# Compression's inputs loaded ahead, and the late modulation's rows on another queue

## The chip, the cores and the metric

The kernel runs on one core of one Trainium2 chip. The metric is the device time of one execution in microseconds (us); lower is better. Three executions of the kernel before took 2179.93, 2182.69 and 2183.15 us, with a median of 2182.69 us. A difference of under 0.2% can hardly be told from none here.

## The reference

Two transformer blocks follow each other, for one sequence of 512 tokens of width 1024, all in float32. Only the first block's mixer matters for the change. In short:

```python
mod = silu(c) @ ada_w + ada_b                     # 6 x 1024 numbers for the whole sequence
sh_m, sc_m, g_m, sh_f, sc_f, g_f = split(mod, 6)
h = rmsnorm(x, norm_g[0]) * (1 + sc_m) + sh_m
p = h @ w_in                                      # 1024 -> all mixers' inputs
y_a = rwkv7_mix(...)                              # a recurrent scan, 4 heads
y_b = fox_mix(...)                                # causal attention, 6 heads
y_c = nsa_mix(...)                                # attention over compressed, chosen and near keys, 6 heads
    # inside: for t in (kc, vc): blocks of 32 tokens, a step of 16, so 31 blocks
    #   flat = (block + pe).reshape(31, 2 groups, 2048); t_cmp = gelu(flat @ w1) @ w2
y = concat([y_a, y_b, y_c]) @ w_out
x = x + g_m * rmsnorm(y, norm_g[1])
h = rmsnorm(x, norm_g[2]) * (1 + sc_f) + sh_f     # the feed-forward block follows
```

The first two of the six parts of `mod` are needed at once. The other four (`g_m`, `sh_f`, `sc_f`, `g_f`), called the late modulation here, are needed only when the mixer's output is added to x.

## The kernel before, in words

Activations lie transposed in SBUF: 128 features on the partitions, 512 tokens along them. TensorE's products are made in three passes of split float32 (`whi`, `wlo` against `uh`, `ul`). The weights come as one stream of blocks of 128x1024 numbers (512 KB): `Weights.load` (L263) takes one of three buffers `raw` and loads it on SP's queue, and `Weights.next` (L273) splits it into `whi` (ScalarE, L278) and `wlo` (VectorE, L279), after which the buffer is free.

The program is written as Python generators that are stepped in turn. At build time a planner then orders the instructions of every engine: it takes them by their place in the program, and a later one ahead of an earlier one when its buffers and inputs are ready by the planner's own reckoning. On the chip each engine, and SP's queue of loads too, works through its list in that fixed order. So a load that is written late and waits for nothing can stand early.

The stages around the change:

- **The first stage** (0 to about 73 us) makes the early modulation and the first projection (L527 to L604). Its loads run on SP's queue (L531, L558, L269).
- **prep** (L750) makes the recurrent scan's inputs for two halves, t = 0 and 1, and between its steps the first `NA` = 5 projections are filled in (L1163 to L1165), among them `kcv[0]` and `kcv[1]`, the inputs of compression.
- **The core stage** (L1179 to L1193) steps the two scans (`core`, L823) 32 times. In each turn it fills in about 2.2 projection steps (L1183) from the other ten projections, takes three steps (L1187) of a side list (compression, then the three pairs of fox heads, then `stacks`), and in every second turn calls `some_ada` (L1186).
- **some_ada** (L621) does one of 16 rows of the late modulation: two loads of 512 KB on SP's queue into `raw`, the same three buffers that the weights use (L630, L631), then on GpSimd four multiplications and additions for each (L635, L637, L638) into `am`. One row later two small products with ones on TensorE (L644) and an addition (L646) finish a row. `some_ada(99)` (L1193) finishes what is left.
- **compress** (L1013) works for keys, then values. For each of two groups it copies a part of `kcv` into `kk2`, shifted by one token in the lower half (L1020, L1021, on SP's queue), and VectorE adds the position term into `kr` (L1025). Four loads of `w1` of 256 KB (L1029) each serve four products (L1032). All of `kr`, `kk2` and `w1` take the five buffers called `e` of the scan.
- **The selected and window attention** (`nsa`, L1217) follows, and the first part of the output projection is filled in between its steps.

The late results `ks`, `kw` and `nq0` to `nq2` (L509, L510) and `fq`, `fk` (L515) have tiles of their own in the pool `keep`, which exist from the start, although they are written only by the last projections of the core stage.

Of the kernel before, what the change touches and what calls it, by code (L numbers as in the profile page):

```python
# [255 lines left out]
class Weights:  # L256


    def __init__(self, nc, pool, src, raw_bufs, bufs):
        self.nc, self.pool, self.src, self.raw_bufs, self.bufs = nc, pool, src, raw_bufs, bufs  # L260
        self.i = 0
# [22 lines left out]
def two_blocks(ctx, tc, ins, out):  # L284
# [224 lines left out]
    ks, kw = [keep.tile([P, T], F32, name=n) for n in ("ks", "kw")]  # L509
    nq = [keep.tile([P, T], F32, name=f"nq{j}") for j in range(3)]  # L510
# [4 lines left out]
    fq, fk = [[keep.tile([P, T], F32, name=f"f{c}{j}", tag=f"f{c}{j}") for j in range(3)] for c in "qk"]  # L515
# [104 lines left out]

    def some_ada(n=1):  # L621

        for _ in range(n):
            if not todo and not owing:
                return
            if todo:
                sec, k = todo.pop(0)
                am = st.tile([P, 256], F32, name="am", bufs=4)
                for q in range(2):
                    aw = wpool.tile([P, 4, 256], F32, name="raw", bufs=W.raw_bufs)  # L630
                    nc.sync.dma_start(aw.rearrange("p a b -> p (a b)"), ins["ada"][sec, k][:, q * 1024:(q + 1) * 1024])  # L631
                    for r in range(4):
                        s = sil[:, 4 * q + r:4 * q + r + 1]
                        if q + r == 0:
                            G.tensor_scalar(am, aw[:, r], s, 1.0, op0=MUL, op1=MUL)  # L635
                            continue
                        G.tensor_scalar(aw[:, r], aw[:, r], s, 1.0, op0=MUL, op1=MUL)  # L637
                        G.tensor_tensor(am, am, aw[:, r], op=ADD)  # L638
# [310 lines left out]
    def copy_to(dst, scale=1.0):  # L949
        return lambda ps: act(dst, ps, AF.Copy, scale=scale)  # L950
# [3 lines left out]
    jobs = [proj_t("nsa", copy_to(kcv[0])), proj_t("nsa", copy_to(kcv[1])), proj_n("nsa_n", 280, 2, evac_n),  # L954
            proj_n("fox_n", 384, 2, lambda b, ps: act(fv[:, b], ps, AF.Copy))]
    for j in range(3):
        jobs += [proj_t("fox", copy_to(fq[j], -0.125)), proj_t("fox", copy_to(fk[j]))]
    jobs += [proj_t("nsa", copy_to(t)) for t in (ks, kw)] + [proj_t("nsa", copy_to(t, -0.125)) for t in nq]
# [54 lines left out]
    def compress(spare):  # L1013

        for j, nm in enumerate(("k", "v")):
            pe = vc("pe_" + nm, 0, 16)
            krs = [spare("kr") for _ in range(2)]
            for g in range(2):
                kk = spare("kk2")
                nc.sync.dma_start(kk[0:64], kcv[j][H2[g]])  # L1020
                nc.sync.dma_start(kk[64:128, :T - 1], kcv[j][H2[g], 1:])  # L1021
                kv = kk.rearrange("p (c j l) -> p c j l", j=8, l=2)[:, :, :, 0].rearrange("p c j -> p j c")
                for a in range(2):
                    kr = krs[a][:, :496].rearrange("p (j g c) -> p j g c", g=2, c=31)
                    tt(kr[:, :, g], kv[:, :, a:a + 31], pe[:, 8 * a:8 * a + 8, None].to_broadcast([P, 8, 31]), ADD)  # L1025
            ps = bank("a", 1)
            for q in range(4):
                w1 = spare("w1")
                nc.sync.dma_start(w1, ins[f"c{nm}1"][:, q * T:(q + 1) * T])  # L1029
                for a in range(4):  # L1030
                    yield
                    mm(ps[:, :62], w1[:, a * P:(a + 1) * P], krs[q // 2][:, (4 * (q % 2) + a) * 62:(4 * (q % 2) + a + 1) * 62],  # L1032
                       q + a == 0, q + a == 6)
# [90 lines left out]
    def fox(j, spare):  # L1124
# [7 lines left out]
        for i in range(NB):  # L1132
# [3 lines left out]
            for s in range(2):  # L1136
                ps = pS()
                mm(ps[:, :n], fq[j][H2[s], qs], fk[j][H2[s], :n], True, False)
# [11 lines left out]
        evac(fq[j], po)  # L1150

    def stacks(spare):
# [4 lines left out]
        for src, tiles in ((ks, ka[:4]), (kw, [ka[4], *(kb[:, i] for i in range(3))])):  # L1157
# [5 lines left out]
    for t in range(2):  # L1163
        for _ in prep(t):
            fill(FP)  # L1165
    for _ in work[0]:
# [10 lines left out]
    turn = [0]  # L1177
    cores = [core(t) for t in range(2)]
# [14 lines left out]
    some_ada(99)  # L1193
    phA.close()
# [22 lines left out]
    def nsa(j):  # L1217
        po = None
        q2 = stack_q(nq[j])
# [5 lines left out]
        for i in range(NB):  # L1225
# [3 lines left out]
            for s in range(2):  # L1229
                h = j + 3 * s  # L1230
                ps = pS()
                mm(ps[:, :31], nq[j][H2[s], qs], kct[H2[s]])
# [26 lines left out]
        evac(nq[j], po)  # L1259
        return nq[j]  # L1260

    us = [split(y, k) for k, y in enumerate((*ya, *fq))]
# [822 lines left out]
```

## Time and profile before

| | before |
|---|---|
| median of three executions | 2182.69 us |
| profiled execution, whole | 2181.48 us |
| its span, first to last instruction | 2179.7 us |
| TensorE busy | 2132.7 us (98%) |
| VectorE, ScalarE, GpSimd busy | 1138.9, 788.5, 478.3 us |
| mean granted TensorE clock | 0.984 of full speed |

The page divides the span into 40 slices of 54.5 us; the core stage lies in the third to the seventh. TensorE's busy time counts a product from its issue to its end, with products overlapping, so 98% does not say that TensorE runs at its full rate. The granted clock is given as a share of full speed: 1.0 is 2.4 GHz and 0.5 is 1.2 GHz. "Idle before, and what ended it" and the chain of waits are worked out from semaphore events.

### The profile page before, as it was taken

To read this page: it belongs to the slowest core of one execution; us is meant where nothing else is said; L and a number is where in the kernel's file an instruction comes from. 1 tells how busy PE (TensorE), PEld (TensorE's weight loads), DVE (VectorE), ACT (ScalarE), POOL (GpSimd) and SP (SyncE) were. 2 spreads that over 40 slices of the span, in tenths; PEclk is the share of its full clock that TensorE was granted. 3 is DMA by queue.
4 is the path that set the end of the run, shared out by engine and by line. 5 is a ranking of instruction groups with operands and counts; after the bars stand their busy time and mean duration, and the time that the engine had idled before them with its cause. 6 is when DMAs were issued, how large, how long until landed. Compare 5 with 4: busy or idle time off the path is not lost.

```text
span 2179.7 us, 31765 instructions
## 1 busy us (share of the span) xinstructions
PE 2132.7 (98%) x12546; PEld 1762.0 (81%) x12546; DVE 1138.9 (52%) x2195; ACT 788.5 (36%) x1342; POOL 478.3 (22%) x523
## 2 busy tenths in 40 slices
PE   7989999999999999899999999999999999999999
PEld 5877777667788888888888899998877888888887
DVE  6653444667752664643344449957554455433442
ACT  4422223553542443432222335455353233222221
POOL 3169661232000000020011024333221022100110
PEclk9989998998999999999999999999999999999999
DMA  8344334102532223122222343342342222222222
GB/s 308 103 133 160 119 132 136 54 31 83 181 106 98 97 97 114 64 91 97 97 97 97 126 147 107 109 129 73 110 140 86 97 92 94 96 96 98 98 98 84
DMA packets 84848, 238.32 MB, mean 109 GB/s; under 512 B 13971, under 2 KB 21449, under 8 KB 84571
## 3 DMA queue, kind: packets, MB, share of 16 engines
q1 hardware_dynamic: 78874, 226.19, 31.3%
q0 software_dynamic: 5104, 9.52, 1.2%
q8 instruction: 99, 1.62, 0.3%
q10 hardware_dynamic: 720, 0.57, 0.1%
q14 instruction: 51, 0.41, 0.1%
HBM read 216.02 MB, written 15.33 MB: 106 GB/s over the span
## 4 chain that ended last, share of the span: by engine, by line
PE 90%; POOL 4%; DMA 3%; DVE 2%; issue 1%; ACT 1%; SPq 0%; POOLq 0%; DVEq 0%; ACTq 0%
PE mm L288 69%; PE psm L288 4%; PE pS L288 3%; PE psr L288 2%; PE k L288 2%; DMA raw<-in_ada_dram 2%; POOL am L638 2%; PE pO L288 2%; PE pso L288 2%; PE pss L288 2%; POOL raw L637 1%; PE pT L1670 1%; PE pst L1101 1%; DMA raw<-in_wst_dram 1%; PE pT L1653 1%
## 5 line engine op out<-in xcount | busy, mean ns | idle before, releaser
L278 ACT ACTIVATE whi<-raw 128x1024 fp32r<-128x1024 f32 (+4 forms) x310 | 323.4, 1046 | 821.6 <-PE mm L288 615.6
L279 DVE TENSOR_TENSOR wlo<-raw,whi 128x1024 fp32r<-128x1024 f32 (+4 forms) x301 | 366.2, 1218 | 332.7 <-ACT whi L278 332.1
L288 PE MATMUL mm<-uh,wlo 128*128 128x512 f32 (+1 forms) x1264 | 488.3, 387 | 0.2 <-DVE wlo L279 0.2
L288 PE MATMUL mm<-uh,whi 128*128 128x512 f32 (+1 forms) x1264 | 485.7, 387 | 2.5 <-DVE gg L294 2.3
L288 PE MATMUL mm<-ul,whi 128*128 128x512 f32 (+1 forms) x1264 | 487.7, 386 | 0.0
L288 PEld LDWEIGHTS mm<-uh,whi 128*128 128x128 f32 x1264 | 237.7, 188 | 50.7 <-DVE gg L294 2.6
L288 PEld LDWEIGHTS mm<-uh,wlo 128*128 128x128 f32 x1264 | 238.3, 188 | 49.2 <-DVE wlo L279 1.0
L288 PEld LDWEIGHTS mm<-ul,whi 128*128 128x128 f32 x1264 | 238.3, 189 | 47.5 <-issue 0.2
L288 PE MATMUL mm<-hh,wlo 128*128 128x512 f32 (+1 forms) x550 | 209.3, 381 | 0.0
L288 PE MATMUL mm<-hl,whi 128*128 128x512 f32 (+1 forms) x550 | 209.3, 381 | 0.0
L288 PE MATMUL mm<-hh,whi 128*128 128x512 f32 (+1 forms) x550 | 208.4, 381 | 0.0
L1519 POOL TENSOR_TENSOR gg<-gg,R 128x512 f32<-128x512 f32 x44 | 76.3, 1737 | 474.3 <-ACT gg L291 474.3
L288 PE MATMUL mm<-whi,uh 128*128 128x256 f32 (+1 forms) x488 | 140.5, 288 | 0.0
L288 PE MATMUL mm<-whi,ul 128*128 128x256 f32 (+1 forms) x488 | 139.8, 287 | 0.0
L288 PE MATMUL mm<-wlo,uh 128*128 128x256 f32 (+1 forms) x488 | 139.2, 285 | 0.0
L288 PEld LDWEIGHTS mm<-hl,whi 128*128 128x128 f32 x550 | 103.4, 188 | 19.9
L288 PEld LDWEIGHTS mm<-hh,wlo 128*128 128x128 f32 x550 | 103.4, 188 | 19.8
L288 PEld LDWEIGHTS mm<-hh,whi 128*128 128x128 f32 x550 | 103.4, 188 | 19.6
L291 ACT ACTIVATE p<-p,smin 128x128 f32<-128x128 f32 (+4 forms) x136 | 81.8, 602 | 92.0 <-DVE smin L1077 52.3
L294 DVE TENSOR_TENSOR gh<-mm,gg 128x512 f32<-128x512 f32 x44 | 30.4, 692 | 132.1 <-PE mm L288 128.5
L288 PEld LDWEIGHTS mm<-whi,ul 128*128 128x128 f32 x488 | 93.2, 191 | 1.7 <-issue 1.5
L366 POOL TENSOR_TENSOR rr<-rv,mhalf 128x4 f32<-128x4 f32 (+1 forms) x6 | 8.8, 1466 | 390.4 <-DVE rv L298 390.4
(536 smaller groups left out, 3553.6 us busy)
## 6 DMA issues: line engine op xcount, KB each, us to landing
raw<-in_wst_dram SPq DMA_DIRECT2D x294, 512.0 KB
raw<-in_ada_dram SPq DMA_DIRECT2D x32, 512.0 KB
aw<-in_ada_dram SPq DMA_DIRECT2D x16, 512.0 KB
raw<-in_wst_dram SPq DMA_DIRECT2D x8, 448.0 KB
ka<-d POOLq DMA_DIRECT2D x1, 3570.0 KB, 49.8
k<-d POOLq DMA_DIRECT2D x1, 2556.0 KB, 17.4
part<-in_x_dram SPq DMA_DIRECT2D x4, 512.0 KB
xa<-in_x_dram SPq DMA_DIRECT2D x8, 256.0 KB
```

Of the source, the lines that this page charges most:

```text
L278: nc.scalar.activation(hi[:, :n], w, AF.Copy)
L279: (e or nc.vector).tensor_tensor(lo[:, :n], w, hi[:, :n].bitcast(F32), op=ALU.subtract)
L288: PE.matmul(o, l, r, start=start, stop=stop)
L291: S.activation(o, i, f, **kw)
L294: V.tensor_tensor(o, a, b, op=op)
L366: G.tensor_tensor(r[:, :n], v[:, :n], mhalf[:, :n], op=ALU.pow)
L637: G.tensor_scalar(aw[:, r], aw[:, r], s, 1.0, op0=MUL, op1=MUL)
L638: G.tensor_tensor(am, am, aw[:, r], op=ADD)
L1101: PE.transpose(ps[:, j:j + P], p[:, j:j + P], ident)
L1519: G.tensor_tensor(g, g, R, op=MUL)
L1653: PE.transpose(ps[:, (j * nb + b) * P:(j * nb + b + 1) * P], xn[:, (b * n + j) * P:(b * n + j + 1) * P], ident)
L1670: PE.transpose(ps[:, j:j + P], p[:, o + j:o + j + P], ident)
```

## The change

Four edits come together:

- **Compression's inputs ahead.** Seven tiles `ahead` take the places (`tag`) of results that come late: nq0, nq1, nq2, kw, ks, fk2, fq2. Right after prep's first half the eight copies of `kcv` and the first three quarters of the keys' `w1` are written to SP's list, into these places.
- **compress without its own loads in step.** The position term is added by `keys(j)` straight from `ahead`. The other five quarters of `w1` are loaded into the places that the copies leave, two after `keys(0)` and three after `keys(1)`, which itself comes at the keys' third quarter.
- **Late tiles made when first written.** `own` and `fox_in` make the tiles ks, kw, nq, fq2 and fk2 when their projection is written out, since their places are in use before.
- **The late modulation on GpSimd's queue.** A row is loaded in four quarters of 256 KB (128 rows of 2 KB) instead of two halves, by DMAs that GpSimd issues, into two halves of one buffer `raws`; the next quarter's load is issued ahead of the arithmetic on this one. From the start of the core stage's loop to `some_ada(99)` the weights use only the other two buffers `raw`; before and after it every third weight load uses `raws`.

```diff
@@ Weights @@
-        raw = self.pool.tile([P, 1024], F32, name="raw", bufs=self.raw_bufs)
+        last = self.spare and self.n % self.raw_bufs == self.raw_bufs - 1
+        self.n += 1
+        raw = self.pool.tile([P, 1024], F32, name="raws" if last else "raw", bufs=1 if last else self.raw_bufs - 1)
@@ two_blocks @@
-    ks, kw = [keep.tile([P, T], F32, name=n) for n in ("ks", "kw")]
-    nq = [keep.tile([P, T], F32, name=f"nq{j}") for j in range(3)]
+    ahead = [keep.tile([P, T], F32, name="ahead", tag=t) for t in ("nq0", "nq1", "nq2", "kw", "ks", "fk2", "fq2")]
+    nsat = {}
+    def own(n):
+        if n not in nsat:
+            nsat[n] = keep.tile([P, T], F32, name=n, tag=n)
+        return nsat[n]
...
+    def pieces():
+        ax = wpool.tile([P, 4, 256], F32, name="raws", bufs=1)
+        order = [(sec, k, q) for sec in (1, 2) for k in range(8) for q in range(4)]
+        def load(i):
+            sec, k, q = order[i]
+            h = ax[:, 2 * (i % 2):2 * (i % 2) + 2]
+            G.dma_start(h.rearrange("p a b -> p (a b)"), ins["ada"][sec, k][:, q * 512:(q + 1) * 512])
+            return h
+        h = load(0)
+        for i in range(len(order)):
+            nxt = load(i + 1) if i + 1 < len(order) else None
+            yield h
+            h = nxt
+    rows = pieces()
...
-                for q in range(2):
-                    aw = wpool.tile([P, 4, 256], F32, name="raw", bufs=W.raw_bufs)
-                    nc.sync.dma_start(aw.rearrange("p a b -> p (a b)"), ins["ada"][sec, k][:, q * 1024:(q + 1) * 1024])
-                    for r in range(4):
+                for q in range(4):
+                    h = next(rows)
+                    for r in range(2):
                         # the multiplications and additions on G are as before, on h[:, r]
...
     def compress(spare):
+        krs = {}
+        def keys(j):
+            krs[j] = [spare("kr") for _ in range(2)]
+            # for both groups: kr = shifted view of ahead[2 * j + g] + pe, as before
+        def weights(j, q, t):
+            w1 = keep.tile([P, T], F32, name="w1", tag=t)
+            nc.sync.dma_start(w1, ins["c" + "kv"[j] + "1"][:, q * T:(q + 1) * T])
+            return w1
+        keys(0)
+        ws = ahead[4:] + [weights(0, 3, "nq0"), weights(1, 0, "nq1")]
         for j, nm in enumerate(("k", "v")):
-            # kk2 loaded from kcv (two DMAs a group), kr made, w1 loaded a quarter at a time
             for q in range(4):
+                if j == 0 and q == 2:
+                    keys(1)
+                    ws += [weights(1, i, t) for i, t in ((1, "nq2"), (2, "kw"), (3, "ks"))]
+                w1 = ws[4 * j + q]
...
     for t in range(2):
         for _ in prep(t):
             fill(FP)
+        if t == 0:
+            for j in range(2):
+                for g in range(2):
+                    nc.sync.dma_start(ahead[2 * j + g][0:64], kcv[j][H2[g]])
+                    nc.sync.dma_start(ahead[2 * j + g][64:128, :T - 1], kcv[j][H2[g], 1:])
+            for q in range(3):
+                nc.sync.dma_start(ahead[4 + q], ins["ck1"][:, q * T:(q + 1) * T])
...
+    W.spare = False                                # ahead of the core stage's loop
...
     some_ada(99)
+    W.spare = True
```

The remaining edits only replace the names ks, kw, nq, fq and fk by `own(...)` and `fox_in(...)`.

## Rows read from the trace of the kernel before

**Rows 1.** Windows, core 0: us, each engine's busy us (x instructions), PEclk, DMA share, GB/s.

```profile
113.00:195.00 82.00, 70.30 (x711) 60.07 (x712) 38.42 (x61) 22.03 (x34) 61.73 (x91) 0.83 0.49 150
195.00:345.00 150.00, 146.38 (x1896) 110.25 (x1897) 66.25 (x171) 43.01 (x94) 92.56 (x151) 1.00 0.37 128
```

**Rows 2.** The same view in steps of 10 us, where the clock fell.

```profile
145.00:155.00 10.00, 7.15 (x54) 5.91 (x52) 4.69 (x7) 0.00 (x0) 8.88 (x14) 0.79 0.62 180
155.00:165.00 10.00, 9.38 (x96) 8.05 (x98) 4.83 (x8) 1.71 (x3) 7.71 (x11) 0.52 0.78 246
...
175.00:185.00 10.00, 5.90 (x70) 4.99 (x64) 3.62 (x10) 1.23 (x3) 9.17 (x14) 0.83 0.62 187
185.00:195.00 10.00, 10.00 (x116) 8.47 (x116) 1.39 (x2) 3.83 (x6) 8.09 (x16) 0.83 0.48 163
```

**Rows 3.** Timeline of PE: start, us, instruction [idle before <- releaser].

```profile
149.91 3.18 PE L288 MATMUL psa<-kr,w 128*128 128x62 f32 x16 [2.71 <-DMA w<-in_ck_dram]
...
157.82 1.51 PE L288 MATMUL psa<-kr,w 128*128 128x62 f32 x6 [0.62 <-DMA w<-in_ck_dram]
...
162.81 0.63 PE L288 MATMUL psm<-uh,wlo 128*128 128x512 f32 x1
...
167.16 0.39 PE L288 MATMUL psm<-uh,wlo 128*128 128x512 f32 x1
...
181.37 0.31 PE L288 MATMUL psa<-ch,w 128*64 128x31 f32 x4 [4.10 <-DVE ch L294]
```

**Rows 4.** Waits from 113 to 235 us: who <- for whom: us, times, longest.

```profile
ACT whi L278 <- DMA raw<-in_wst_dram: 46.0, 6, 21.1
...
DVE kr L294 <- DMA kk<-kcv: 11.7, 2, 7.9
```

**Rows 5.** Chain of waits from 110 to 240 us: start, us, what.

```profile
198.62 3.26 DMA raw<-in_wst_dram
...
204.66 3.86 DMA raw<-in_ada_dram
```

**Rows 6.** GpSimd's groups from 113 to 365 us: busy us, mean ns | idle before.

```profile
L638 POOL TENSOR_TENSOR am<-am,raw 128x256 f32<-128x256 f32 x112 | 87.3, 789 | 4.7
L637 POOL TENSOR_SCALAR raw<-raw,sil 128x256 f32<-128x256 f32 x112 | 57.4, 529 | 27.2 <-DMA raw<-in_ada_dram 27.1
L635 POOL TENSOR_SCALAR am<-raw,sil 128x256 f32<-128x256 f32 x16 | 9.5, 593 | 24.8 <-DMA cf<-in_cmat_dram 13.3 <-PE psr L288 6.3 <-DMA raw<-in_ada_dram 3.2
```

**Rows 7.** The tile am from 113 to 365 us: ns min/median/max, first and last start.

```profile
L638 POOL TENSOR_TENSOR am<-am,raw x112: 717/728/1718, 131.1 to 322.6; 128x256 f32<-128x256 f32 x112
...
L288 PE MATMUL psr<-ones,am x64: 164/250/373, 156.4 to 361.2; 128*128 128x1 f32 x64
L635 POOL TENSOR_SCALAR am<-raw,sil x16: 473/482/1333, 128.1 to 316.6; 128x256 f32<-128x256 f32 x16
```

**Rows 8.** GpSimd's own DMA issues, whole span: busy us, mean ns.

```profile
L499 POOL DMA_DIRECT2D k<-d x2 | 2.3, 1126 | 7.7 <-DMA d<-lo 7.7
...
L468 POOL DMA_DIRECT2D l<-in_lines_dram x1 | 0.6, 570 | 0.0
```

**Rows 9.** DMA issues on the page: KB each, median us to landing.

```profile
rb<-in_rel_bias_dram POOLq DMA_DIRECT2D x1, 0.8 KB, 5.7
l<-in_lines_dram POOLq DMA_DIRECT2D x1, 210.4 KB, 7.0
```

**Rows 10.** Waits from 235 to 365 us.

```profile
POOL hr L733 <- DVE hv L298: 24.0, 2, 22.8
```

**Rows 11.** Timeline of SP in the first stage.

```profile
0.73 2.27 SPq L531 DMA_DIRECT2D part<-in_x_dram  x4
...
16.24 0.33 SPq L1036 DMA_DIRECT2D w<-in_nsa_ck_w_dram  x1
```

**Rows 12.** Windows of the first stage and of prep, columns as in the first group.

```profile
10.00:20.00 10.00, 8.00 (x43) 4.06 (x43) 5.10 (x10) 4.28 (x9) 3.81 (x4) 1.00 1.03 416
...
85.00:100.00 15.00, 15.00 (x106) 13.55 (x105) 7.26 (x12) 4.25 (x8) 1.67 (x1) 1.00 0.23 80
```

More of the change, by code (lines that the diff above doesn't have):

```diff
@@ L514, in two_blocks, with fox_in @@
     fv = keep.tile([P, NB, 384], F32, name="fv", tag="fv")
-    fq, fk = [[keep.tile([P, T], F32, name=f"f{c}{j}", tag=f"f{c}{j}") for j in range(3)] for c in "qk"]
+    fqk = {}
+    def fox_in(n):
+        if n not in fqk:
+            fqk[n] = keep.tile([P, T], F32, name=n, tag=n)
+        return fqk[n]
+    for n in ("fq0", "fk0", "fq1", "fk1"):
+        fox_in(n)
     kcv = [keep.tile([P, T], F32, name=f"kcv{j}", tag=f"kcv{j}") for j in range(2)]
@@ L949, in copy_to @@
     def copy_to(dst, scale=1.0):
-        return lambda ps: act(dst, ps, AF.Copy, scale=scale)
+        return lambda ps: act(dst(), ps, AF.Copy, scale=scale)
     LO = 0
     FP, FN, NS, FC, NA, OR, AE = 1.6,2.4,3,(2.2,2.6),5,0,2
-    jobs = [proj_t("nsa", copy_to(kcv[0])), proj_t("nsa", copy_to(kcv[1])), proj_n("nsa_n", 280, 2, evac_n),
+    jobs = [proj_t("nsa", copy_to(lambda: kcv[0])), proj_t("nsa", copy_to(lambda: kcv[1])), proj_n("nsa_n", 280, 2, evac_n),
             proj_n("fox_n", 384, 2, lambda b, ps: act(fv[:, b], ps, AF.Copy))]
     for j in range(3):
-        jobs += [proj_t("fox", copy_to(fq[j], -0.125)), proj_t("fox", copy_to(fk[j]))]
-    jobs += [proj_t("nsa", copy_to(t)) for t in (ks, kw)] + [proj_t("nsa", copy_to(t, -0.125)) for t in nq]
+        jobs += [proj_t("fox", copy_to(lambda j=j: fox_in(f"fq{j}"), -0.125)), proj_t("fox", copy_to(lambda j=j: fox_in(f"fk{j}")))]
+    jobs += [proj_t("nsa", copy_to(lambda n=n: own(n), 1.0 if n[0] == "k" else -0.125)) for n in ("ks", "kw", "nq0", "nq1", "nq2")]
     def project(jobs):
@@ L1013, in compress @@
     def compress(spare):
[L1015 to L1025 removed]
+        krs = {}
+        def keys(j):
+            pe = vc("pe_" + "kv"[j], 0, 16)
+            krs[j] = [spare("kr") for _ in range(2)]
+            for g in range(2):
+                kv = ahead[2 * j + g].rearrange("p (c j l) -> p c j l", j=8, l=2)[:, :, :, 0].rearrange("p c j -> p j c")
+                for a in range(2):
+                    kr = krs[j][a][:, :496].rearrange("p (j g c) -> p j g c", g=2, c=31)
+                    tt(kr[:, :, g], kv[:, :, a:a + 31], pe[:, 8 * a:8 * a + 8, None].to_broadcast([P, 8, 31]), ADD)
+        def weights(j, q, t):
[4 more added lines that the diff above has]
+        ws = ahead[4:] + [weights(0, 3, "nq0"), weights(1, 0, "nq1")]
+        for j, nm in enumerate(("k", "v")):
             ps = bank("a", 1)
             for q in range(4):
[L1028 to L1029 removed]
+                if j == 0 and q == 2:
+                    keys(1)
+                    ws += [weights(1, i, t) for i, t in ((1, "nq2"), (2, "kw"), (3, "ks"))]
+                w1 = ws[4 * j + q]
                 for a in range(4):
                     yield
[L1032 removed]
+                    mm(ps[:, :62], w1[:, a * P:(a + 1) * P], krs[j][q // 2][:, (4 * (q % 2) + a) * 62:(4 * (q % 2) + a + 1) * 62],
                        q + a == 0, q + a == 6)
@@ L1156, in stacks @@
         kb = keep.tile([P, 3, T], F32R, name="ksw3", tag="fv")
-        for src, tiles in ((ks, ka[:4]), (kw, [ka[4], *(kb[:, i] for i in range(3))])):
+        for src, tiles in ((own("ks"), ka[:4]), (own("kw"), [ka[4], *(kb[:, i] for i in range(3))])):
             kst.append(stack_k(src, tiles, *(spare("s" + c, F32R) for c in "hl")))
@@ L1165, in two_blocks @@
             fill(FP)
+        if t == 0:
+            for j in range(2):
+                for g in range(2):
+                    nc.sync.dma_start(ahead[2 * j + g][0:64], kcv[j][H2[g]])
+                    nc.sync.dma_start(ahead[2 * j + g][64:128, :T - 1], kcv[j][H2[g], 1:])
+            for q in range(3):
+                nc.sync.dma_start(ahead[4 + q], ins["ck1"][:, q * T:(q + 1) * T])
     for _ in work[0]:
@@ L1218, in nsa @@
         po = None
-        q2 = stack_q(nq[j])
+        q2 = stack_q(own(f"nq{j}"))
         tbs = []
@@ L1231, in nsa @@
                 ps = pS()
-                mm(ps[:, :31], nq[j][H2[s], qs], kct[H2[s]])
+                mm(ps[:, :31], own(f"nq{j}")[H2[s], qs], kct[H2[s]])
                 p = att.tile([P, 31], F32, name="pc", bufs=2)
@@ L1258, in nsa @@
                         mm(po[H2[s], qs], nv[:, kb, c:c + 64], pts[s][:, kb * P:(kb + 1) * P], False, b == 2 and kb == i)
-        evac(nq[j], po)
-        return nq[j]
-    us = [split(y, k) for k, y in enumerate((*ya, *fq))]
+        evac(own(f"nq{j}"), po)
+        return own(f"nq{j}")
+    us = [split(y, k) for k, y in enumerate((*ya, *(fox_in(f"fq{j}") for j in range(3))))]
     def project_out():
```

21 lines of the change are left out of this document (12 added, 9 removed).

## The prediction

> **What bounds the kernel now.** I read the page first: TensorE is counted busy for 98% of the span, so only a stretch in which it idles or runs at the lower clock has anything to give. The windows of the core stage say where [rows 1]: from 113 to 195 us TensorE is busy for 70.3 of 82 us at a granted clock of 0.83, from 195 to 345 us for 146.4 of 150 us at 1.00. The finer windows [rows 2] show the two bad spots, 145 to 165 us and 175 to 195 us, where the clock falls to as little as 0.52, that is, where TensorE is mostly at 1.2 GHz. The timeline of PE names what came ahead of each fall [rows 3]: 2.71 us in which the first products of compression wait for `w1`, and 4.10 us in which its closing products wait for VectorE's `ch`. VectorE in turn has stood still for 11.7 us for two copies `kk` [rows 4]; those stand in SP's list among loads that wait for a free buffer. The chain of waits says why such buffers are scarce [rows 5]: a weight load of 512 KB is issued as GpSimd lets go of a buffer, and the next load of modulation rows as VectorE does. ScalarE stands for 46.0 us before its split of a weight block for this [rows 4], nearly all of it beside a busy TensorE. So the bound is TensorE throughout, behind a short queue of late loads in the first third of the stage.
>
> **The change part by part.** The base of the sum is the profiled execution, 2181.48 us (span 2179.7 us and 1.8 us around it), 1.2 us below the median of 2182.69 us.
>
> *Compression's waits.* The copies and three quarters of `w1` are written to SP's list about 40 us ahead of their use, into places that nothing holds. The 2.71 and 0.62 us for `w1` go. Of the 4.10 us for `ch`, the part for `kk` goes; VectorE's and ScalarE's own short sequence between the sums and the closing product remains, so I count 3.1 of it. Together 2.7 + 0.6 + 3.1 = 6.4 us (bounds 3.3, if `ch` stays as late as it is, and 7.4).
>
> *The lower clock.* In the four windows the clock's shortfall is 0.21, 0.48, 0.17 and 0.17 of 10 us, 10.3 us in all [rows 2]. The same pass takes 0.63 us inside and 0.39 us outside [rows 3]. If the two gaps go, TensorE has worked on without a break and should keep 2.4 GHz. The bounds are 0 (the scan's steps on VectorE and ScalarE set the pace, or a new gap takes the place) and 10.3. VectorE is busy for 4.8 and ScalarE for 1.7 of the worst 10 us, so they leave room, but the scan is a chain of short steps over three engines. I take 6.5 us.
>
> *Weights with two buffers of their own.* SP's list loses 32 loads of modulation rows, and the blocks arrive ahead of need. TensorE is busy anyway after 195 us, with 3.6 us idle in 150 [rows 1]; I take 1.0 us of that (bounds 0 and 3.6).
>
> *GpSimd's list.* Arithmetic is unchanged: 87.3 + 57.4 + 9.5 = 154.2 us [rows 6], 2.41 us for one of 64 quarters. New are 64 issues. GpSimd's own issues here cost 0.57 and 1.13 us [rows 8], the first for 33 long rows, the second for hundreds of short ones; 128 rows of 2 KB are nearer to the first, so 0.75 us, 48 us in all (bounds 36 and 72). A quarter is issued ahead of the arithmetic of the one before it and of one more issue, so its landing is covered for 2 x 0.75 + 2.41 = 3.9 us. A block of 512 KB on SP's queue lands 3.26 us after its issue where little else runs, and half-rows of the modulation take 3.86 [rows 5]; half the bytes should land in about 3 to 4.5 us. I allow 12 us of stalls over 64 quarters (bounds 0 and 150, below). GpSimd begins at 128.1 us [rows 7], since the buffer comes free when it does now, and ends at 128 + 154 + 48 + 12 = 342 us, where it now begins its last addition at 322.6. That lies beside TensorE's work: the products that take up the last `am` come at 361.2 us now [rows 7], about 349 us after the gains. The margin is 7 us, and every microsecond beyond it is a microsecond of the stage, because TensorE's list, the PSUM banks of the next stage and the next weight load into `raws` all stand behind it.
>
> What is queued behind GpSimd's new waits: the scans' two last roots (`hr`, L733), for which GpSimd now stands free 22.8 us ahead [rows 10]. They can find a quarter's wait and arithmetic ahead of them, and the scan's end waits for both. I charge 2.0 us (bounds 0 and 2 x 4).
>
> A rule speaks against this part. GpSimd's additions take 789 ns in the mean [rows 6] against a median of 728 [rows 7], so something holds them up by some 8% now. The Trainium skill, page "SBUF — State Buffer", section "SBUF: two separate sides", says that GpSimd cannot write the descriptors of its DMAs while VectorE runs an operation in a two-port mode, and gives about 620 ns alone against about 3100 ns for one such DMA. By its figures an estimate of 2.5 us more for each of 64 loads would be 160 us at the very worst, if every load met such an operation; no row here shows a load of this kind in this stage.
>
> *The first stage.* A load that waits for nothing is moved far up by the planner: `w2` of compression is issued at 16.24 us [rows 11]. So the three quarters of `w1`, 786 KB, may go there too, where the DMA engines are full (1.03, 416 GB/s [rows 12]): 1.9 us of their time. TensorE waits there mostly for other engines, so I charge 0.5 (bounds 0 and 1.9). The eight copies need `kcv` and fall into prep, with the DMA engines at 0.23 [rows 12]: nothing; if they had no such cover, 1 MB at 416 GB/s would be 2.5 us.
>
> Sum: -6.4 - 6.5 - 1.0 + 2.0 + 0.5 = -11.4 us, 2170.1 us for the profiled execution, and with the 1.2 us to the median 2171 us. With the bounds of these terms but for the landing: -7.4 - 10.3 - 3.6 = -21.3 (2161) to -3.3 + 8 + 1.9 = +6.6 (2189).
>
> **The rivals.**
>
> *A. GpSimd's row of quarters becomes the bound (slower).* With two halves of a buffer, two quarters take a landing L and one arithmetic, so one takes (L + 2.41)/2 when L is over 3.9 us, and the last ends at 128 + 32(L + 2.41). It passes the present last use, 361 us, when L is over 4.9 us; from there the kernel is slower. For it: GpSimd's only two loads from DRAM into SBUF landed 5.7 and 7.0 us after their issue [rows 9], and a stage with 512 KB blocks on the other queue shares the DMA engines. Against it: those two were issued as four x loads, 2 MB, were under way [rows 11], and blocks on SP's queue land in 3.3 to 3.9 us [rows 5]. At 5.7 us the last quarter ends at 388 us, 27 us past the present end: 2183 + 27 = 2210 us. At 7.0 us it is 429 us and 2251 us. The rule of the page above would act here, as a longer L.
>
> The same skill, page "DMA: Bandwidth & Descriptors", section "Anatomy of one DMA — SWDGE (gpsimd) path", fits 2.0 us plus bytes by 436 GB/s, an estimate of 2.6 us for a quarter; by that L stays below 3.9 us and rival A fails.
>
> *B. The scan sets the pace (no change).* If VectorE's and ScalarE's steps of the scan follow each other as late as now, TensorE idles elsewhere, the clock falls there, and what is left is 2 to 4 us, which the roots give back: 2182 us. For it: TensorE is idle for 11.7 us in the first window although ten projections are at hand to fill it [rows 1]. Against it: both gaps name compression, not the scan [rows 3].
>
> *C. More than counted.* With loads never late, the whole first window runs like the second, at 1.00 and with 2.4% idle: 82 us would shrink by up to 11.7 - 2.0 + 0.17 x 82 x 0.8 = 20.9 us, and nothing is given back: 2162 us.
>
> **How the numbers follow.** Forecast 0.48 (2163 to 2178, all faster), A 0.28 (2188 to 2255), B 0.16 (2178 to 2188), C 0.08 (2155 to 2163). A measurement of this kernel tells about 0.2%, 4.4 us, from no change. Faster: the forecast, C and a sixth of B, 0.58. Same: most of B and an edge of A, 0.15. Slower: the rest of A, 0.27. For 8 times in 10 the range leaves out the upper half of A (0.14) and the lower half of C (0.04): 2158 to 2208 us. The likeliest one's own range is 2163 to 2178.
>
> **What the new profile would show.** Step one is right if the products `psa<-kr,w` start without idle time for a DMA and VectorE's wait for `kk` is gone; the second, if the granted clock from 145 to 195 us is near 1.00. GpSimd's row is right if its issues take 0.6 to 1.0 us each, its waits for quarters sum to under 30 us, and its last addition comes before 350 us. Rival A would show as GpSimd idle for 1 us and more ahead of most quarters, with `am` ending past 360 us, and TensorE waiting for `psr<-ones,am` or for a weight block in `raws`. B would show the same gaps under other names. I am wrong altogether if the first stage ends over 2 us later, or if the stages after 365 us change their length.

## The result, and the profile after

The changed kernel takes 2216.03 us (median of 4 runs, 2214.38 to 2216.21) against 2181.31 us for the kernel before beside it: ratio 1.0155, 95% interval 1.0143 to 1.0167. It is slower by 34.7 us; the forecast was 2171. Lines 281, 282, 291 and 294 of the kernel after are the helpers that were 278, 279, 288 and 291; the products and additions of the modulation are L674 and L675 (were L637, L638), the first product of a section (one of the 16 rows, four quarters) L672, the new issue L646, the scans' root L770.

Windows of the kernel after, columns as in [rows 1]. The first two answer to [rows 1]; the third is what follows them.

```profile
113.00:195.00 82.00, 71.12 (x848) 60.83 (x849) 41.37 (x65) 23.07 (x35) 56.08 (x78) 0.88 0.34 118
195.00:345.00 150.00, 137.65 (x1584) 102.78 (x1582) 59.30 (x160) 37.02 (x85) 114.10 (x190) 0.93 0.30 103
345.00:400.00 55.00, 32.79 (x266) 22.74 (x265) 19.42 (x43) 12.54 (x24) 30.11 (x44) 0.66 0.49 150
```

The same last window of the kernel before:

```profile
345.00:400.00 55.00, 54.68 (x259) 39.81 (x261) 29.77 (x88) 20.16 (x51) 13.61 (x15) 0.84 0.50 134
```

The first window, where nearly all the gain was to be, has gained 0.8 us of busy time and 0.05 of the clock. The loss stands behind it: 8.7 us of busy time in the second window, 21.9 in the third. What PE waited for from 113 to 400 us (us in total, times, longest):

```profile
PE psr L291 <- ACT y L294: 22.0, 1, 22.0
PE psr L291 <- POOL am L675: 15.7, 3, 8.0
PE psa L291 <- DVE kr L297: 4.0, 1, 4.0
```

These are 41.7 of the 46.0 us that PE waits there in all. Before, its waits in this stretch were 15.6 us, of which the three of [rows 3] were 7.4. The 30.4 us more are most of the loss; what is left goes with the clock, 0.66 in the third window where it had been 0.84, and is not traced further. The longest is named after ACT's eviction `y`; the timelines of SP and of ACT (start, us, instruction, idle before it and its releaser) say what held that one:

```profile
374.38 0.33 SPq L272 DMA_DIRECT2D raws<-in_wst_dram  x1
```

```profile
355.10 0.62 ACT L294 ACTIVATE sh<-kw 128x512 fp32r<-128x512 f32 x1
378.45 1.06 ACT L281 ACTIVATE whi<-raws 128x1024 fp32r<-128x1024 f32 x1 [22.72 <-DMA raws<-in_wst_dram]
379.41 1.04 ACT L281 ACTIVATE whi<-raw 128x1024 fp32r<-128x1024 f32 x1
380.36 0.58 ACT L294 ACTIVATE y<-psr 128x512 f32<-128x512 f32 x1
```

A weight load into `raws` is issued at 374.38 us, as GpSimd lets go of that place; ACT stands for it with `y` behind it in its list, and PE stands for `y`. So both large entries, 22.0 and 15.7 us, come from one thing: GpSimd's modulation runs late, and ends late. Its groups from 113 to 420 us (busy us, mean ns | idle before), answering to [rows 6]:

```profile
L675 POOL TENSOR_TENSOR am<-am,raws 128x256 f32<-128x256 f32 x112 | 85.4, 763 | 4.3
L674 POOL TENSOR_SCALAR raws<-raws,sil 128x256 f32<-128x256 f32 x112 | 63.8, 576 | 34.8 <-DMA raws<-in_ada_dram 33.9
L646 POOL DMA_DIRECT2D raws<-in_ada_dram x64 | 37.9, 593 | 17.2 <-DVE wlo L282 9.9 <-POOL am L675 7.1 <-issue 0.2
L672 POOL TENSOR_SCALAR am<-raws,sil 128x256 f32<-128x256 f32 x16 | 8.3, 516 | 12.1 <-DMA raws<-in_ada_dram 12.1
```

The last addition starts at 373.6 us, in [rows 7] at 322.6. The arithmetic is about what it was (157.5 us against 154.2), 37.9 us are issues, and 46.0 us are waits for quarters, of which there were to be 12. Yet a quarter lands early, by the page's line on the issues (KB, median us to landing):

```profile
raws<-in_ada_dram POOLq DMA_DIRECT2D x64, 256.0 KB, 2.9
```

A landing of 2.9 us was covered for 3.9 us in the forecast. The timeline of GpSimd shows what really stands between issue and use:

```profile
187.10 0.94 POOL L674 TENSOR_SCALAR raws<-raws,sil 128x256 f32<-128x256 f32 x2 [1.17 <-DMA raws<-in_ada_dram]
187.99 0.74 POOL L675 TENSOR_TENSOR am<-am,raws 128x256 f32<-128x256 f32 x1
189.03 0.59 POOL L646 DMA_DIRECT2D raws<-in_ada_dram  x1 [0.30 <-POOL am L675]
189.65 1.54 POOL L675 TENSOR_TENSOR am<-am,raws 128x256 f32<-128x256 f32 x2
192.02 0.48 POOL L674 TENSOR_SCALAR raws<-raws,sil 128x256 f32<-128x256 f32 x1 [0.82 <-DMA raws<-in_ada_dram]
192.45 0.59 POOL L646 DMA_DIRECT2D raws<-in_ada_dram  x1
193.09 0.48 POOL L674 TENSOR_SCALAR raws<-raws,sil 128x256 f32<-128x256 f32 x1
193.53 1.55 POOL L675 TENSOR_TENSOR am<-am,raws 128x256 f32<-128x256 f32 x2
195.51 0.48 POOL L672 TENSOR_SCALAR am<-raws,sil 128x256 f32<-128x256 f32 x1 [0.43 <-DMA raws<-in_ada_dram]
```

The issue of 189.03 comes behind both products of the quarter that landed before, and behind the last addition that read the half it overwrites, for which it stands 0.30 us. Left to cover the landing are its own 0.59 us and two additions, some 2.2 us. The products of one quarter have run ahead; the next one's find nothing, as their data are 2.9 us away. A wait for a quarter comes 48 times, 0.96 us in the mean.

### The profile page after: what moved, and what is told of

It reads as the page before. It is cut to its first block, busy times and chain, and to the rows that moved or that the text cites. A ratio compares the mean times of both kernels' runs of the same rounds, so it can differ in the third digit from the quotient of the medians.

```text
span 2214.2 us, 31769 instructions
## 1 busy us (share of the span) xinstructions
PE 2135.2 (96%) x12546; PEld 1763.0 (80%) x12546; DVE 1140.4 (52%) x2195; ACT 788.4 (36%) x1342; POOL 516.6 (23%) x587
## 4 chain that ended last, share of the span: by engine, by line
PE 83%; DMA 7%; POOL 5%; issue 2%; DVE 2%; ACT 1%; POOLq 0%; DVEq 0%; ACTq 0%
PE mm L291 67%; DMA raws<-in_ada_dram 7%; PE pS L291 3%; PE psm L291 2%; POOL raws L674 2%; PE k L291 2%; PE pO L291 2%; PE pso L291 2%; POOL am L675 1%; PE pT L1726 1%; PE pss L291 1%; PE pst L1148 1%; PE psr L291 1%; PE pT L1709 1%; PE pT L291 0%
## 5 line engine op out<-in xcount | busy, mean ns | idle before, releaser
L281 ACT ACTIVATE whi<-raw 128x1024 fp32r<-128x1024 f32 (+2 forms) x211 | 220.3, 1046 | 528.1 <-PE mm L291 414.7
L282 DVE TENSOR_TENSOR wlo<-raw,whi 128x1024 fp32r<-128x1024 f32 (+3 forms) x205 | 250.7, 1223 | 220.5 <-ACT whi L281 215.3
L281 ACT ACTIVATE whi<-raws 128x1024 fp32r<-128x1024 f32 (+2 forms) x99 | 103.6, 1047 | 277.6 <-PE mm L291 196.9
L282 DVE TENSOR_TENSOR wlo<-raws,whi 128x1024 fp32r<-128x1024 f32 (+3 forms) x96 | 117.0, 1219 | 112.9 <-ACT whi L281 112.9
L291 PEld LDWEIGHTS mm<-hh,whi 128*128 128x128 f32 x550 | 103.4, 188 | 19.8
L291 PEld LDWEIGHTS mm<-hh,wlo 128*128 128x128 f32 x550 | 103.4, 188 | 19.8
L297 DVE TENSOR_TENSOR gh<-mm,gg 128x512 f32<-128x512 f32 x44 | 30.4, 692 | 132.1 <-PE mm L291 128.5
```

The costliest lines, as they stand in the source:

```text
L281: nc.scalar.activation(hi[:, :n], w, AF.Copy)
L282: (e or nc.vector).tensor_tensor(lo[:, :n], w, hi[:, :n].bitcast(F32), op=ALU.subtract)
L291: PE.matmul(o, l, r, start=start, stop=stop)
L297: V.tensor_tensor(o, a, b, op=op)
```

## The experiments

The theory after this reading: a product writes back into its quarter, so the half is in use until the *addition* is done; the planner places the issue behind that addition, with too little work left to cover the landing; GpSimd's list ends at 374 us, and sections, roots and a weight block hang on it. Rivals: the compression's move, too few buffers for the weights, a late landing. All ratios are to the kernel before, with 95% intervals.

**The compression's half alone.** The modulation is loaded as before, by halves on SP through the weights' buffers.

```diff
-                for q in range(4):
-                    h = next(rows)
+                for q in range(2):
+                    aw = wpool.tile([P, 4, 256], F32, name="raw", bufs=W.raw_bufs)
+                    nc.sync.dma_start(aw.rearrange("p a b -> p (a b)"), ins["ada"][sec, k][:, q * 1024:(q + 1) * 1024])
...
```

> Compression's half of the change alone; the late modulation stays on SP's queue in three shared buffers, as before. Theory (GpSimd's row of quarters ends too late and holds the stage): this half has nothing to do with it, its two gaps of 2.7 and 4.1 us shrink to the one of 4.0 us seen at 139 us, so 2170 to 2182 us. Rival 1 (the early copies and the bundled position terms cost more than they save): 2195 us or more. Rival 2 (two weight buffers are too few): not touched here, 2170 to 2182 us.

Measured: 2181.94 us, 0.9995 [0.9985, 1.0004]: no change. It neither makes the loss nor brings the 6.4 us. PE's two idle times of some length from 148 to 186 us:

```profile
158.57 0.79 PE L288 MATMUL psm<-uh,whi 128*128 128x512 f32 x1 [8.17 <-ACT fk L291]
183.75 1.54 PE L288 MATMUL psa<-kr,w 128*128 128x62 f32 x6 [6.00 <-DVE kct L1074]
```

The waits of [rows 3] are gone, and these two have taken their place. In the first, ACT stands 20.6 us for a weight block with the eviction `fk` behind it: the buffers shared with the modulation's rows are as scarce as before.

**The modulation's half alone.** The compression stays as in the kernel before.

```diff
-                kv = ahead[2 * j + g].rearrange("p (c j l) -> p c j l", j=8, l=2)[:, :, :, 0].rearrange("p c j -> p j c")
+                kk = spare("kk2")
+                nc.sync.dma_start(kk[0:64], kcv[j][H2[g]])
+                nc.sync.dma_start(kk[64:128, :T - 1], kcv[j][H2[g], 1:])
+                kv = kk.rearrange("p (c j l) -> p c j l", j=8, l=2)[:, :, :, 0].rearrange("p c j -> p j c")
...
```

> The late modulation's half alone: quarters on GpSimd's queue, weights in two buffers, compression as before. Theory: GpSimd's last addition again comes at 365 to 380 us and the whole loss is here, 2205 to 2225 us. Rival 1 (compression's move): 2178 to 2190 us. Rival 2 (two weight buffers): also 2205 to 2225 us, but with TensorE and ScalarE waiting for weight loads all through the stage and not for am or the shared buffer.

Measured: 2216.51 us, 1.0156 [1.0131, 1.0182]. The whole loss is here; the last addition starts at 372.0 us.

**Products in a tile of their own.** A half is then free after its last product; `am` gives a buffer for it.

```diff
-                        am = st.tile([P, 256], F32, name="am", bufs=4)
+                        am = st.tile([P, 256], F32, name="am", bufs=3)
...
-                        G.tensor_scalar(h[:, r], h[:, r], s, 1.0, op0=MUL, op1=MUL)
-                        G.tensor_tensor(am, am, h[:, r], op=ADD)
+                        t = st.tile([P, 256], F32, name="amt", bufs=1)
+                        G.tensor_scalar(t, h[:, r], s, 1.0, op0=MUL, op1=MUL)
+                        G.tensor_tensor(am, am, t, op=ADD)
```

> The changed kernel, but each product goes into a tile of its own, so a half of the buffer is free after its second multiplication and the next load is issued ahead of a whole quarter's arithmetic. Theory: a quarter then costs 2.4 us of arithmetic and 0.6 us of issue, some 3.1 to 3.4 us instead of 3.85, GpSimd's last addition comes at 325 to 348 us instead of 374, and the time is 2172 to 2190 us. Rival 2 (two weight buffers): the order on GpSimd does not matter, 2210 to 2220 us. Rival 3 (the loads themselves land late): waits stay near 46 us and the time above 2205 us.

Measured: 2184.65 us, 1.0008 [0.9998, 1.0019]. Where the products go decides the loss: the weights still have two buffers, and a quarter still lands after 2.9 us, so neither of these rivals makes it. GpSimd's waits for quarters (us, times, longest) are 19.8 us instead of 46.0, on 22 occasions instead of 48:

```profile
POOL amt L675 <- DMA raws<-in_ada_dram: 11.9, 17, 1.4
POOL am L672 <- DMA raws<-in_ada_dram: 7.9, 5, 2.6
```

The last addition starts at 359.7 us, later than the theory said (348 at most) and still 37 us later than before, and PE still pays once:

```profile
354.52 1.11 PE L776 MATMUL psr<-cm,nr 128*128 128x128 f32 x4 [10.00 <-DVE nr L773]
```

`nr` needs the scan's root, and the two roots stand at 352 to 356 us in GpSimd's list, behind quarters.

**The quarters issued on SP**, products in place.

```diff
-            G.dma_start(h.rearrange("p a b -> p (a b)"), ins["ada"][sec, k][:, q * 512:(q + 1) * 512])
+            nc.sync.dma_start(h.rearrange("p a b -> p (a b)"), ins["ada"][sec, k][:, q * 512:(q + 1) * 512])
```

> The changed kernel, but the 64 quarters are issued on SP's queue; buffers and arithmetic as in the changed kernel. Theory: GpSimd loses 38 us of issues and the 7 us of waits ahead of them, and an issue no longer stands behind a multiplication that waits; its last addition comes at 320 to 345 us and the time is 2165 to 2190 us. Rival 2 (two weight buffers): 2210 to 2220 us. Rival 3 (64 issues block the weights in SP's list instead): GpSimd ends early but ScalarE waits longer for weight loads, 2185 to 2205 us.

Measured: 2197.88 us, 1.0069 [1.0048, 1.0090]. GpSimd has no issues left, waits 69.1 us for quarters (53.3 and 15.8) and still ends earlier, at 344.2 us. What is lost now is lost on SP, by its timeline:

```profile
205.19 27.46 SPq L646 DMA_DIRECT2D raws<-in_ada_dram  x9
...
254.03 7.84 SPq L646 DMA_DIRECT2D raws<-in_ada_dram  x4
261.93 0.42 SPq L1177 DMA_DIRECT2D fb<-dcum  x1
```

Each issue waits for an addition, and `fb` of the forget gate stands behind them; PE is idle 22.25 us up to 267.39. So the theory is right on GpSimd's end and out on the time; it is the third rival's range, with another load held than the weights.

**The weights kept out of `raws` until after the NSA heads.** GpSimd's list as in the change.

```diff
     some_ada(99)
-    W.spare = True
...
+    W.spare = True
     sq = SqSum()
```

> The changed kernel, with the weights kept out of the tile raws until after the NSA heads, so that no weight load waits for the last quarter. In the changed kernel GpSimd's additions end at 374.4 us and the PE stands 22.0 us up to 381.0, the PE's queue then has products, 5.2 us long, before the next that needs a section (386.2). Theory (GpSimd's late end holds this stage by two ways, the weight load behind it being only the longer one): the passes before the section's product run at once, and the PE then waits for the last additions at about 374 to 376 us, so that 6 to 12 us come back: 2204 to 2210 us. Rival 1 (the weight load alone is the loss, the sections and roots would not hold the stage): about 22 us come back: 2194 us. Rival 2 (two buffers for the weights for longer than before cost as much as the wait): 2216 us, no change. GpSimd's end itself is not to move (372 to 376 us) by any of them.

Measured: 2211.85 us (2205.21 to 2215.09), 1.0127 [1.0107, 1.0148]: by the ratios 0.0028 or 6 us better, the least that the theory allowed (its median is 2 us above the theory's range, and the two intervals still meet at 1.0143 to 1.0148). The wait for the block is gone, and little has come back: the weight block is not the only way. PE's longest wait from 340 to 400 us in the profile, that of the fastest run, and its cause in GpSimd's timeline:

```profile
PE psr L775 <- DVE nr L772: 18.2, 1, 18.2
```

```profile
372.96 3.28 POOL L770 TENSOR_TENSOR hr<-hv,mhalf 128x8 f32<-128x8 f32 x2
```

The two roots stand behind the last quarter, and hold PE instead of the weight block.

**No loads.** Only the first two quarters are loaded; 62 of 64 are left out, so the modulation's numbers are not the reference's. All arithmetic stays.

```diff
-            G.dma_start(h.rearrange("p a b -> p (a b)"), ins["ada"][sec, k][:, q * 512:(q + 1) * 512])
+            if i < 2:
+                G.dma_start(h.rearrange("p a b -> p (a b)"), ins["ada"][sec, k][:, q * 512:(q + 1) * 512])
```

> The changed kernel with only the first two of the 64 quarters loaded; the arithmetic on GpSimd and all other work is the same, and the modulation's numbers are then not the reference's. It shows what the change gives if issue and landing cost GpSimd nothing. Theory (the loss is the 38 us of issues and 53 us of waits that the loads put into GpSimd's list): the last addition ends at 310 to 325 us as in the kernel before, the 22.0 us wait near 359 us is gone, and so are the waits of the PE for GpSimd's sections; the 4.0 us wait at 143 us stays: 2168 to 2180 us. Rival 1 (the weights' two buffers in this stage, or the compression's earlier additions, cost by themselves): 2190 to 2210 us with GpSimd ending by 325 us. Rival 2 (no cost and no gain beside GpSimd): 2182 us.

Measured: 2173.51 us, 0.9957 [0.9940, 0.9974], the last addition at 316.3 us. As the theory expected: without the loads' cost in GpSimd's list the kernel is where the forecast put it, within 3 us. The traffic of the 62 loads is gone here too; the run with own products and quarters on SP, below, has it and takes 2174.99 us.

**No loads, and the compression as before.** The edit above on the modulation's half alone.

> The modulation's half of the change alone, the compression as in the kernel before, and only the first two of the 64 quarters loaded (the modulation's numbers are then not the reference's). Beside the run with the whole change and no loads (2173.51 us, 8.5 us under the kernel before) it tells which part the gain is from. Theory (the compression's early loads are worth about the 6.4 us that the prediction gave them, but only where the modulation's rows no longer share the weights' buffers and SP's list): 2178 to 2182 us. Rival (the gain is that of the weights' loads freed of the modulation's rows, and the compression's move gives nothing, as it gave nothing alone): 2172 to 2175 us.

Measured: 2167.69 us, 0.9933 [0.9913, 0.9953]. My theory here expected 2178 to 2182 and is out: with the modulation's rows away, the old compression does as well as the moved one, or better. The windows of 113 to 145 us, first with the compression moved, then as before:

```profile
113.00:145.00 32.00, 23.89 (x149) 20.07 (x150) 22.66 (x33) 12.58 (x19) 19.56 (x22) 0.85 0.28 87
```

```profile
113.00:145.00 32.00, 28.96 (x201) 24.09 (x203) 24.05 (x33) 12.70 (x19) 19.64 (x27) 0.89 0.35 107
```

In these 32 us PE is busy for 5.1 us less with the move, and 4.4 of them are a wait that the move brings with it, in the changed kernel too. DVE's and then PE's timeline of the changed kernel:

```profile
141.46 3.87 DVE L297 TENSOR_TENSOR kr<-ahead,vec 128x248 f32<-128x248 f32 x8
```

```profile
142.99 1.11 PE L291 MATMUL psa<-kr,ahead 128*128 128x62 f32 x4 [4.02 <-DVE kr L297]
```

As all four inputs are there, the planner does the eight key additions in one piece, and takes the products that need them early; PE stands for the first. With loads that come one by one, the additions come in twos between other work. But behind this stretch the old compression has a wait of its own, 3.3 us for `ch` (1.7 with the move), and a lower clock, again with the move first:

```profile
165.00:195.00 30.00, 27.11 (x475) 23.87 (x474) 15.87 (x20) 7.63 (x12) 29.68 (x47) 1.00 0.07 22
```

```profile
165.00:195.00 30.00, 26.74 (x359) 23.54 (x357) 14.58 (x17) 5.16 (x9) 30.00 (x50) 0.77 0.19 55
```

So the place of this cost is shown, and that it makes the difference between the two runs is argued only. The two intervals meet at 0.994 to 0.995, so the size of that difference, about 5 us, is not sure either.

**Own products, weights late.** The two edits named so together.

> The run with the products in a tile of their own, and the weights kept out of raws until after the NSA heads as well. Without the second edit that kernel had a 10.0 us wait of the PE at 344 us for the scans' roots, which stand behind quarters on GpSimd, and then 2.4 us for a weight eviction behind the last quarter. Theory: only the 2.4 us can come back, and two buffers for longer take about as much: 2180 to 2185 us. Rival (the weight loads behind raws also hold SP's list, and so other loads): 2172 to 2179 us.

Measured: 2186.21 us, 1.0017 [1.0007, 1.0026]. A miss by 1 us, and nothing gained: the wait for `nr` is 14.0 us here, since the roots still follow the quarters, and the last addition still starts at 358.9.

**The last rows on DVE.** Own products, and for three of 16 sections one instruction on DVE in place of two on GpSimd.

```diff
+                        if sec == 2 and k > 4:
+                            stt(am, h[:, r], s, am, MUL, ADD)
+                            continue
```

> The run with the products in a tile of their own, and for the last three of the 16 sections (21 rows) product and addition in one instruction on DVE in place of two on GpSimd. Theory (what is left of the loss is GpSimd's late end, 359.7 us, with the scans' roots behind it): GpSimd's list loses 21 times 1.34 us, 28 us, and ends at 328 to 338 us; the PE's 10.0 us wait at 344 us is gone and DVE pays some 8 us beside the PE's work: 2172 to 2180 us. Rival 1 (DVE is in the scans' loop, and waits there for the rows to land): 2184 to 2192 us. Rival 2 (the 10 us wait has another cause and stays): 2184 us.

Measured: 2186.75 us, 1.0021 [1.0010, 1.0032]. The theory is out, and rival 1 is right: the 10 us wait for `nr` is down to 1.1, but DVE, in the scans' loop, stands 12.1 us for GpSimd and then seven times for a quarter, and PE stands 6.5 us for `NF` behind it. DVE's timeline:

```profile
315.55 0.48 DVE L306 SCALAR_TENSOR_TENSOR am<-raws,sil,am 128x256 f32<-128x256 f32 x1 [12.14 <-POOL am L672]
```

**Own products, quarters issued on SP.** The two edits shown above.

> The changed kernel with the products in a tile of their own and the quarters issued on SP in place of GpSimd. Measured for the two edits alone: 2184.65 us (issue on GpSimd, 38.0 us in its list, last addition at 359.7) and 2197.88 us (SP, 53.3 and 15.8 us of waits for landings, since an issue waits for the addition before last). Theory (landing is hidden once an issue waits only for the product, and the issue's 38 us are what is left of the loss): between the last product of one quarter and the first product of the quarter after the next GpSimd has some 3.4 us of work of its own, more than a landing of 2.3 to 3 us, so its waits fall under 15 us, its last addition ends at 318 to 332 us, and with the waits of the PE gone the time goes to the ceiling of the run without the loads, 2173.5 us: 2171 to 2178 us. Rival 1 (SP's list: an issue that waits for GpSimd still holds the load of the forget gate's sums, and so the PE): 2184 to 2198 us. Rival 2 (the landings beside the weights' loads are later than 3.4 us): waits over 40 us, 2182 to 2190 us.

Measured: 2174.99 us, 0.9963 [0.9952, 0.9975]: faster than both kernels, and 1.5 us from the run without loads. The last addition starts at 329.5 us. SP's issues now wait only for products, and PE has no long wait for `fb` or for the roots. GpSimd's waits for quarters are 22.7 us, more than the 15 of the theory:

```profile
POOL am L672 <- DMA raws<-in_ada_dram: 14.6, 5, 12.5
POOL amt L675 <- DMA raws<-in_ada_dram: 8.1, 9, 3.1
```

**The same on ACT's queue** (`nc.scalar.dma_start`).

> The same with the quarters issued on ACT's queue. What an issue costs ACT no run here shows; 64 of them at GpSimd's 0.59 us would be 38 us of an engine that is busy for some 78 of 195 us before 310 us. Theory: GpSimd's list ends at 318 to 332 us as with SP, and an issue that waits for a product holds evictions behind it on ACT for up to some 2 us at a time, of which the PE sees a part: 2175 to 2186 us. Rival (ACT's evictions are what the PE waits for most in this stage, and 64 waits there cost more than GpSimd's issues did): 2190 to 2210 us.

Measured: 2189.66 us, 1.0033 [1.0019, 1.0048]. The theory, 2186 us at most, is out; this is the edge of the rival. An issue costs ACT little, but each waits for a product with evictions behind it; the worst place of ACT's timeline:

```profile
146.00 23.22 ACTq L646 DMA_DIRECT2D raws<-in_ada_dram  x7
169.27 1.06 ACT L281 ACTIVATE whi<-raw 128x1024 fp32r<-128x1024 f32 x1 [24.55 <-POOL amt L675]
```

**Own products, quarters on SP, the compression as before.** To see whether the move costs 5 us there as well.

> The modulation's half alone, its quarters issued on SP and the products in a tile of their own; the compression stays as in the kernel before. The like kernel with the compression moved early took 2174.99 us (ratio 0.9963). Theory (from the two runs without the loads, 2173.51 us with the compression moved and 2167.69 us without: the move costs about 5 us where SP's list is free, since its eight key additions stand in one piece on DVE at 141 us and the PE waits 4.0 to 4.8 us for them): 2167 to 2172 us, without that wait. Rival 1 (with the quarters on SP its list is not free, and the compression's keys wait for their copies as in the kernel before): 2175 to 2180 us. Rival 2 (the difference between the two runs without loads was chance): 2174 to 2176 us.

Measured: 2186.48 us (2180.61 to 2190.74), 1.0019 [1.0009, 1.0030]. The theory is out, rival 1 or worse is right: with the quarters in SP's list the compression's copies and weights are issued late again. SP, then PE:

```profile
143.29 3.12 SPq L632 DMA_DIRECT2D raws<-in_ada_dram  x2
146.46 0.53 SPq L1044 DMA_DIRECT2D kk<-kcv  x1
...
150.40 1.42 SPq L1053 DMA_DIRECT2D w<-in_ck_dram  x2
```

```profile
153.66 2.58 PE L291 MATMUL psa<-kr,w 128*128 128x62 f32 x11 [6.32 <-DMA w<-in_ck_dram]
```

This profile is of one of the fastest runs, 5 us under the median. From 145 to 165 us PE is busy for 13.68 us at a clock of 0.65; with the compression moved it was 20.00 at 0.88. So the compression's move is worth 0.0056, some 12 us, here; it is worth nothing where the rows share the weights' buffers (the first run), and nothing or less without the loads.

## Why the prediction was wrong, step by step

*The step that failed* is in GpSimd's list: "A quarter is issued ahead of the arithmetic of the one before it and of one more issue, so its landing is covered for 2 x 0.75 + 2.41 = 3.9 us." I read that order from the program's text, where `load(i + 1)` stands ahead of the arithmetic on quarter i. But the half that it fills is written by the products of quarter i-1 and read by their additions, on the engine that issues. So the issue comes behind them, and the planner, which had the products of quarter i ready, put those ahead too. The cover was 2.2 us, the landing 2.9, and 46.0 us of waits for landings with 7.1 us of issues that wait for an addition came in place of 12. The run with products of their own, which changes what holds the half, takes, by the ratios, 32 of the 34 us back: shown.

*What hung on it was right in its places and too small.* The margin was said to be 7 us, and every microsecond beyond it one of the stage. The list ended 32 us after 342, which makes 25 us beyond the margin and 2196 us by that rule; the kernel took 20 us more. PE's 15.7 us for sections on the way (3.5 us up to 180 us, 4.1 up to 211, 8.0 up to 319) were in no term, as only the last section was held to matter; with the 4.0 us for `kr` they have that size. The places named, the products of `am`, the roots and the weight block in `raws`, are the three that PE waited for: the products and the block in the change itself, the roots in the runs with own products or with the block spared.

*The other terms of the list.* An issue takes 0.59 us (I took 0.75), 37.9 us in all instead of 48. A quarter lands after 2.9 us, just below the 3 to 4.5 that I gave. The roots at 2.0 us were too cheap as soon as the list is late: 10.0 us with own products, 18.2 with the weights spared. With stalls of 19.8 us, near my 12, the list still ended at 360.4 instead of 342: 8.4 us GpSimd is idle ahead of its additions, and 3.3 us for the roots and 2.6 us for `sl` were not in my sum.

*Rival A* had the right end (2210 us, slower) and nearly all of its signs: GpSimd idle for 0.96 us ahead of 48 quarters, `am` past 360 us, PE waiting for the products of `am` and for the block in `raws`. Its condition was wrong: it was to act from a landing of 4.9 us, and acted at 2.9, as the landing's cover was shorter than in its formula too. The Trainium skill, page "DMA: Bandwidth & Descriptors", section "Anatomy of one DMA — SWDGE (gpsimd) path", gave an estimate of 2.6 us, which the trace nearly bears out (2.9). That rival A fails by such a landing was my inference, and false. The Trainium skill, page "SBUF — State Buffer", section "SBUF: two separate sides", gives such a load about 620 ns alone and about 3100 ns where VectorE's operation keeps GpSimd from writing its descriptors. I had put that on the issues; none of the 64 took over 0.72 us, so this run does not show it:

```profile
L646 POOL DMA_DIRECT2D raws<-in_ada_dram x64: 548/596/721, 124.2 to 369.0; - x64
```

*The compression's waits.* The three waits did go, and 4.0 us came in their place, so 3.4 us remained in the change where I took 6.4, and none in the run that does it alone. The term took each wait as removable by itself. But with the rows out of SP's list and the compression as before (no loads), PE's waits for `w1` fall from 3.3 to 0.4 us and the one for `ch` from 4.1 to 3.3, while moving the loads alone leaves ACT's weight blocks late. So the gains were in part two ways to the same one, and I added them. That the sum's size was nearly right for the whole (8.5 us without loads, against 11.4) is luck: it put 1.0 us on the weights' own buffers and 6.4 on the move, and the run without loads and without the move is 14.6 us under the kernel before by its ratio, faster than with the move.

*The lower clock.* It followed the idle time as said, and so fell elsewhere: 0.86, 1.00, 0.68 and 0.98 in the four windows of [rows 2], 4.8 us of shortfall instead of 10.3, and 0.66 around the 22.0 us wait, where it had been 0.84. *The first stage* cost nothing that shows (PE is busy for 57.0 of its 72 us, before for 57.3). Behind the stage nothing changed: the first products of the projection out start at 395.85 us, before at 362.09, and these 33.8 us are all but 0.7 of the difference between the two profiled executions.

What stays open: what the move of the compression costs by itself where SP is free (about 5 us, intervals that touch, the cause argued), and whether key additions held back for j = 1 would remove that; it was not tried.

## What to carry to other kernels

When a load is issued from the queue of the engine that uses the data, work out its cover from the last instruction that touches its place, reads of in-place results included, not from where the call stands in the program; one more tile for the result can be worth more than a better queue. A load that must wait belongs on a queue where nothing urgent stands behind it, and its waits are to be made short first: the same quarters cost 69 us of waits for landings on SP with products in place, 22.7 us with products apart. Two edits that empty the same list are not added: price the second with the first already done.

## What the runs showed of the hardware

The issue of a 256-KB load took 0.59 us of GpSimd and 0.33 us of ACT or SP where it did not wait. An issue behind an addition of the same engine that it depends on started 0.30 us after the end of it, 24 times. An engine's DMA issues that wait are shown on its queue's rows as long entries (23.22 us for seven on ACT), not as its busy time: the group of evictions there seems to wait for GpSimd's product, while it is the issue ahead of it that does.
